# More seven-product quads, one weight split by an adding transfer, and a head that reads x already turned

## The chip, the cores and the metric

The kernel runs on one core of a Trainium2 chip. TensorE (PE) multiplies, VectorE (DVE), ScalarE (ACT) and GpSimd (POOL) work on tiles, SyncE (SP) issues most of the loads. The metric is the device time of one execution in microseconds. Three runs of the kernel before gave 2032.25, 2032.9 and 2036.04 us; the median is 2032.9 us.

## The reference, cut to what matters

One layer works on x of 256 tokens by 2048 numbers, in fp32. It has three stages, each of them a residual step:

```python
f = _swiglu(_rmsnorm(h, ln_ffn1_pre), ffn1_gate, ffn1_up, ffn1_down)   # (silu(u@gate) * (u@up)) @ down
h = h + 0.5 * _rmsnorm(f, ln_ffn1_post)
mx = _hybrid_mixer(_rmsnorm(h, ln_mix_pre), w_in, ..., w_out)          # RWKV branch, pooling branch, two gates
h = h + _rmsnorm(mx, ln_mix_post)
f = _swiglu(_rmsnorm(h, ln_ffn2_pre), ffn2_gate, ffn2_up, ffn2_down)
h = h + 0.5 * _rmsnorm(f, ln_ffn2_post)
```

The hidden width of both feed-forward stages is 5632, so gate and up are 2048 x 5632 and down is 5632 x 2048. The mixer reads x through `w_in` and ends with `w_out` (2048 x 2048).

## The kernel before, in words

**Three products for one.** Every fp32 matrix is used as a high and a low part of type fp32r. ACT casts a loaded weight tile `w` to its high part (`wH<-w`), DVE subtracts the high part from the tile (`wL<-w,wH`). The helper `mm3` (L264 to L266) then issues three matmuls of 128 x 128 by 128 x 512 for each product of a row block and a weight tile: high by high, high by low, low by high. The 256 tokens are two halves of 128, the accumulators are PSUM banks of 128 x 512.

**Pairs and quads.** A pair (`pair` in `seven`, fed by `feed`, L281 cast and L287 subtraction) is two k-tiles of one 512-column weight block for both halves: 4 products, 12 matmuls. A quad (`quad`, lines L506 to L534) takes two k-tiles of two column blocks at once, which would be 8 products, and computes them with 7 after Strassen and Winograd, 21 matmuls. For that it needs sums of weight tiles (`t<-w,w` L513, `t<-w,t` L517 and L521 on DVE, split into high and low at L530 and L534) and sums of the activations (`sums`, tiles `sf`, `sH`, `sL`), which are made once and used by all column blocks. Four products go into banks of their own (p1, p5, p6, p7, shown as `ms`), which `merge` adds into the results (`u<-ms,u` and `u<-mm,u`, L570).

**Which k-tiles are quads** is written in strings: `FAST` for each of the nine gate/up blocks (blocks 2 to 10 of 11; blocks 0 and 1 are plain), `DOWN` for the two column pairs of down, `OUT` for the pair of columns 1 and 2 of `w_out`. In a string, f is a plain pair of the first column block, l one of the last, q a quad.

**A planner sets the order.** `job`, `pe`, `run` and `play` hold a list of jobs with a duration, a due time and dependencies, play them once with the written durations while the program is built, and write the instructions of PE, ACT and DVE in the order that comes out. Loads go to SP's queue, the moves of the hidden tiles (`x<-T`, 16 per block) to POOL's. Staging tiles for loads (`w32`, four of them) and pairs of split tiles (`wH`, `wL`, five) are handed on in the plan: the next user waits until the job that gives a tile free is done. The hidden tiles of a gate/up block are gated by DVE (L905), turned in 32 x 32 pieces (L786), moved by POOL and at once cast and split (L809 on ACT, L813 on DVE) into `xH` and `xL`.

**The head.** The first block loads x in token layout; PE turns it (`tr<-ident,x`, L768, four 128 x 128 transposes at a time, after 12 transposes `warm<-ident`), ACT and DVE scale and split it out of PSUM. The vectors of gains are loaded in rows and turned by PE too (`pg`, `pr`). Part of the work that follows (`gemm_rest`, `gemm_tok`, the first half of `ev_pa`) is not in the plan; its order is left to the scheduler.

Of the kernel before, what the change touches and what calls it, by code (L numbers as in the profile page):

```python
# [18 lines left out]
P = 128  # L19
D = 2048  # L20
S = 256
# [19 lines left out]
WARM = 12  # L41
# [13 lines left out]
ROWS = [("ln_mix_pre", 16), ("ln_ffn2_pre", 16), ("mu", 26), ("w0", 8), ("a0", 8),  # L55
        ("k_k", 8), ("k_a", 8)]
ROWS2 = [("r_k", 8), ("gn_w", 8), ("gn_b", 8), ("pool_scale", 8)]
# [18 lines left out]
class Block:  # L76
# [43 lines left out]
    def job(s, eng, dur, fn, due=0.0, deps=(), take=None, give=(), lag=None,  # L120
            rel=0.0):
        s.n += 1
        n = Node(s.n, eng, dur, fn, due, LAG[eng] if lag is None else lag, give)
        n.ready = rel if eng != "D" else rel - 10
        for d in deps:
            s.link(d, n)
        if take:
            s.asks.setdefault(take, []).append(n)
        if eng != "P":
            s.jobs.append(n)  # L130
        return n
# [14 lines left out]
    def run(s):  # L146
# [3 lines left out]
        for name, ns in s.asks.items():  # L150
            ns.sort(key=lambda n: n.due)
            wait[name] = deque(ns[CAPS[name]:])
            for n in wait[name]:
                n.left += 1
        order = deque(n for _, n in sorted(s.order, key=lambda o: o[0]))
        with s.tc.manual_schedule(engines={E.PE, E.Activation, E.DVE}):
            s.play(order, wait)
            s.stats()
        s.clk, s.order, s.asks, s.freed, s.jobs = 0.0, [], {}, {}, []

    def play(s, order, wait):

        free = dict(P=0.0, A=0.0, V=0.0, G=0.0, D=-10.0)
# [17 lines left out]
        def done(n, t):  # L181
            for name in n.give:
                if wait.get(name):
                    met(wait[name].popleft(), t)
# [83 lines left out]
    def feed(s, w, k, n, c0, t, hold=False):  # L268
# [3 lines left out]
        def get():  # L272
            b["w"] = s.get_w(w, k, n, c0, 512)

        def high():
            if hold:
                b["H"], b["L"] = s.unit(dt=F32R, p="kH"), s.unit(dt=F32R, p="kL")
            else:
                b["H"], b["L"] = [s.wp.tile([P, 1024], F32R, tag=g, name=s.nm(g), bufs=WS_BUFS)
                                  for g in ("wH", "wL")]  # L280
            s.nc.scalar.copy(b["H"][:, :m], b["w"][:, :m])  # L281
# [4 lines left out]
        def low():  # L286
            s.nc.vector.tensor_tensor(out=b["L"][:, :m], in0=b["w"][:, :m],  # L287
                                      in1=b["H"][:, :m].bitcast(F32), op=ALU.subtract)
        g = s.job("D", 1.75 * m / 1024, get, t - 9, take="w")
        h = s.job("A", aa(m), high, t - va(m) - aa(m) - 0.5, (g,), None if hold else "ws")  # L290
        return b, s.job("V", va(m), low, t - va(m) - 0.3, (h,), give=("w",))
# [10 lines left out]
    def gemm(s, w, c0, at, k0, k1, KT, evac, names, kd=lambda k: (), pss=None):  # L302
# [9 lines left out]
        for k in range(k0, k1, 2):  # L312
            b, l = s.feed(w, k, 2, c0, s.clk)
            e = s.pe(12 * MM, lambda k=k, b=b: do(k, b),
                     (l, *kd(k), *kd(k + 1), *(s.open(*names) if k == 0 else ())), ("ws",))
# [4 lines left out]
    def halves(s, w, c0, at, k0, k1, KT, names, pss, kd=lambda k, h: (), ends=None):  # L320

        fed, last = {}, None
        for k in range(k0, k1, 2):
            fed[k] = s.feed(w, k, 2, c0, s.clk + (k - k0) * 3 * MM, k - k0 >= 2 * WS_BUFS)
        for h in range(2):
            for k in range(k0, k1):
                b, l = fed[k // 2 * 2]

                def do(k=k, h=h, b=b):
# [3 lines left out]
                last = s.pe(3 * MM, do, (l, *kd(k, h), *(s.open(names[h]) if k == 0 else ())),  # L333
                            ("ws",) if h and k % 2 and k - k0 < 2 * WS_BUFS else ())
# [3 lines left out]
    def gemm_tok(s, w, c0, at, KT, evac, xs=None):  # L338

        pss = [s.pm.tile([P, 512], F32, tag="mm", name=s.nm("mm")) for _ in range(2)]  # L340
        ws = {}

        def do(k, h):
            (wH, wL), (xH, xL) = ws[k], at(k)
            s.mm3(pss[h], xH[:, h * P:h * P + P], xL[:, h * P:h * P + P], wH, wL,
                  k == 0, k == KT - 1)

        def keep(tiles):
            ws.update((k, (wH, wL)) for k, wH, wL in tiles)

        if xs:
            s.head(w, c0, KT, do, keep, xs)
        else:
            for k2 in range(0, KT, 4):
                keep(s.load_w(w, k2, min(4, KT - k2), c0, 512))
                for k in range(k2, min(k2 + 4, KT)):
                    do(k, 0)
                    do(k, 1)
        with s.tc.high_priority(offset=BOOST):
            for h in range(2):  # L360
                evac(h, pss[h])

    def lead(s, w, c0, at, KT, kd):
# [3 lines left out]
        s.run()  # L367
        return pss

    def gemm_rest(s, w, c0, at, KT, evac, pss):  # L370

        for k2 in range(STAG, KT, 4):
            ws = {k: t for k, *t in s.load_w(w, k2, min(4, KT - k2), c0, 512)}
            for k in range(k2, min(k2 + 4, KT)):
                for h in range(2):
                    (wH, wL), (xH, xL) = ws[k], at(k)
                    s.mm3(pss[f"f{h}"], xH[:, h * P:h * P + P], xL[:, h * P:h * P + P],
                          wH, wL, k == 0, k == KT - 1)
        with s.tc.high_priority(offset=BOOST):
            for h in range(2):  # L380
                evac(h, pss[f"f{h}"])

    def sums(s, src, sm, q0, nq, t, deps, own=None, hl=False):
# [1471 lines left out]
```

## Time and profile before

| | |
|---|---|
| median of three runs | 2032.9 us |
| the profiled execution, its own time | 2033.49 us |
| its span | 2031.8 us |
| PE busy | 2014.8 us (99%) |
| DVE busy | 1735.4 us (85%), 95.69 of the 100 us from 300 to 400 |
| ACT busy | 1164.7 us (57%) |
| POOL busy | 326.6 us (16%) |
| loads and stores | 423.55 MB, mean 208 GB/s |

The span is the stretch that the profiler shows, from the first to the last instruction; 1.7 us of the profiled execution's time lie outside it. Busy shares are of the span. DVE's share is an average over stages: the nine gate/up blocks with quads run from about 97 to 470 us and from about 1421 to 1795 us, down follows each of them, and the mixer lies between.

### The profile page before, as it was taken

How to read it: one execution, taken by the hardware profiler on the slowest of the kernel's cores; microseconds unless marked ns; L12 is line 12 of the kernel's file. 1: busy time of each engine (PE TensorE's matmuls, PEld its weight loads, DVE VectorE, ACT ScalarE, POOL GpSimd, SP SyncE). 2: the span in 40 equal slices, each digit the busy share in tenths (PEclk: the TensorE clock that was granted, in tenths of full speed). 3: DMA queues.
4: the chain of work that ended last, by engine and by line, in shares of the span. 5: the costliest groups of instructions: out<-in, count | busy, mean ns of one | idle time of the engine just before them, and what ended most of it. 6: DMA issues, size and time to landing. Idle time of an engine off the chain costs nothing.

```text
span 2031.8 us, 28759 instructions
## 1 busy us (share of the span) xinstructions
PE 2014.8 (99%) x10011; PEld 1664.1 (82%) x10011; DVE 1735.4 (85%) x2300; ACT 1164.7 (57%) x1559; POOL 326.6 (16%) x673
## 2 busy tenths in 40 slices
PE   9999999999999999999999999999999999999997
PEld 7888888888888888888788788888888878888886
DVE  6989999988998857789689577769999989989986
ACT  7555565555565566685575444565565555555653
POOL 0121112211000023403220111012211122110000
PEclk9999999999999999999999999999999999999999
DMA  7666676766667777757456557676666767666674
GB/s 261 205 198 218 217 220 203 226 201 221 208 207 253 233 210 215 205 176 215 144 176 183 161 171 271 209 219 192 213 211 216 222 190 232 201 221 209 205 258 146
DMA packets 226842, 423.55 MB, mean 208 GB/s; under 512 B 24063, under 2 KB 27529, under 8 KB 226697
## 3 DMA queue, kind: packets, MB, share of 16 engines
q1 hardware_dynamic: 204137, 384.70, 60.8%
q0 software_dynamic: 22272, 36.51, 5.5%
q8 instruction: 78, 1.28, 0.3%
q10 hardware_dynamic: 288, 0.52, 0.1%
q14 instruction: 67, 0.55, 0.1%
HBM read 396.69 MB, written 8.39 MB: 199 GB/s over the span
## 4 chain that ended last, share of the span: by engine, by line
PE 97%; issue 1%; DMA 1%; DVE 1%; ACT 1%; POOL 0%; DVEq 0%; POOLq 0%; SPq 0%; ACTq 0%
PE mm L264 27%; PE mm L266 27%; PE mm L265 27%; PE ms L266 4%; PE ms L265 4%; PE ms L264 4%; PE tr L768 1%; DMA x<-T 0%; PE pA L1575 0%; PE mc L728 0%; PE pU L1671 0%; DMA w<-in_ffn_gate_dram 0%; PE pSa L1683 0%; PE pY L1706 0%; PE pT L1742 0%
## 5 line engine op out<-in xcount | busy, mean ns | idle before, releaser
L264 PE MATMUL mm<-wH,xH 128*128 128x512 f32 (+1 forms) x2232 | 871.6, 391 | 0.0
L266 PE MATMUL mm<-wH,xL 128*128 128x512 f32 (+1 forms) x2232 | 866.5, 388 | 0.6 <-DVE xL L777 0.5
L265 PE MATMUL mm<-wL,xH 128*128 128x512 f32 (+1 forms) x2232 | 866.6, 388 | 0.2
L281 ACT CAST wH<-w 128x1024 fp32r<-128x1024 f32 x373 | 388.1, 1053 | 231.3 <-PE mm L266 139.5
L287 DVE TENSOR_TENSOR wL<-w,wH 128x1024 fp32r<-128x1024 f32 x373 | 449.4, 1221 | 77.8 <-ACT wH L281 72.0
L266 PEld LDWEIGHTS mm<-wH,xL 128*128 128x128 f32 x2232 | 419.0, 188 | 87.9 <-DVE xL L777 2.3
L264 PEld LDWEIGHTS mm<-wH,xH 128*128 128x128 f32 x2232 | 419.1, 188 | 86.4 <-ACT xH L772 0.2
L265 PEld LDWEIGHTS mm<-wL,xH 128*128 128x128 f32 x2232 | 419.3, 188 | 85.1 <-DVE wL L287 1.0
L530 ACT CAST wH<-t 128x1024 fp32r<-128x1024 f32 x172 | 181.1, 1053 | 221.9 <-DVE t L521 113.1
L797 POOL DMA_DIRECT2D x<-T x352 | 173.1, 499 | 735.2 <-issue 299.0
L241 DVE TENSOR_TENSOR wL<-w,wH 128x1024 fp32r<-128x1024 f32 (+3 forms) x178 | 209.9, 1188 | 82.7 <-ACT wH L240 81.2
L240 ACT CAST wH<-w 128x1024 fp32r<-128x1024 f32 (+3 forms) x178 | 182.1, 1027 | 149.7 <-PE mm L266 129.3
L534 DVE TENSOR_TENSOR wL<-t,wH 128x1024 fp32r<-128x1024 f32 x172 | 205.9, 1219 | 14.3 <-ACT wH L530 13.6
L530 ACT CAST wH<-w 128x1024 fp32r<-128x1024 f32 (+1 forms) x172 | 143.1, 834 | 70.7 <-PE mm L266 32.5
L534 DVE TENSOR_TENSOR wL<-w,wH 128x1024 fp32r<-128x1024 f32 (+1 forms) x172 | 163.7, 952 | 5.2 <-ACT wH L530 5.0
L513 DVE TENSOR_TENSOR t<-w,w 128x1024 f32<-128x1024 f32 x86 | 105.0, 1220 | 12.2 <-DMA w<-in_ffn_down_dram 7.6
L570 DVE TENSOR_TENSOR u<-mm,u 128x512 f32<-128x512 f32 x92 | 61.1, 683 | 11.0 <-PE mm L266 11.0
L265 PE MATMUL ms<-wL,sH 128*128 128x512 f32 x174 | 67.9, 390 | 1.4 <-DVE wL L534 1.4
L264 PE MATMUL ms<-wH,sH 128*128 128x512 f32 x174 | 67.8, 390 | 1.0 <-ACT wH L530 1.0
L266 PE MATMUL ms<-wH,sL 128*128 128x512 f32 x174 | 67.7, 389 | 0.0
L570 DVE TENSOR_TENSOR u<-ms,u 128x512 f32<-128x512 f32 x92 | 61.3, 687 | 1.6
L809 ACT CAST xH<-x 128x512 fp32r<-128x512 f32 x44 | 26.8, 617 | 62.4 <-DMA x<-T 59.5
(332 smaller groups left out, 2064.4 us busy)
## 6 DMA issues: line engine op xcount, KB each, us to landing
w<-in_w_in_dram SPq DMA_DIRECT2D x128, 512.0 KB
w<-in_ffn_up_dram SPq DMA_DIRECT2D x122, 512.0 KB
w<-in_ffn_gate_dram SPq DMA_DIRECT2D x120, 512.0 KB
w<-in_ffn_down_dram SPq DMA_DIRECT2D x116, 512.0 KB
w<-in_ffn_down_dram SPq DMA_DIRECT2D x120, 256.0 KB
w<-in_ffn_gate_dram SPq DMA_DIRECT2D x112, 256.0 KB
w<-in_ffn_up_dram SPq DMA_DIRECT2D x108, 256.0 KB
w<-in_w_out_dram SPq DMA_DIRECT2D x28, 512.0 KB
```

The source lines that it names most:

```text
L240: s.nc.scalar.copy(vH, v)
L241: s.nc.vector.tensor_tensor(out=vL, in0=v, in1=vH.bitcast(F32), op=ALU.subtract)
L264: nc.tensor.matmul(ps, aH, bH, start=start, stop=False)
L265: nc.tensor.matmul(ps, aH, bL, start=False, stop=False)
L266: nc.tensor.matmul(ps, aL, bH, start=False, stop=stop)
L281: s.nc.scalar.copy(b["H"][:, :m], b["w"][:, :m])
L287: s.nc.vector.tensor_tensor(out=b["L"][:, :m], in0=b["w"][:, :m], in1=b["H"][:, :m].bitcast(F32), op=ALU.subtract)
L513: V.tensor_tensor(out=v["t13"], in0=v["a"], in1=v["b0"].to_broadcast([P, 2, 512]), op=ALU.subtract)
L530: nc.scalar.copy(x[n_][0], v[n_])
L534: V.tensor_tensor(out=L, in0=v[n_], in1=H.bitcast(F32), op=ALU.subtract)
L570: V.tensor_tensor(out=u[o], in0=pss[b], in1=u[i], op=ALU.add)
L797: nc.gpsimd.dma_start(out=x[0][q * 32:q * 32 + 32, i], in_=src[i * 32:i * 32 + 32, q])
```

## The change

**The strings.** Each gate/up block has four quads in place of three and so four pairs of each column block in place of five. Down's first pair has eight quads in place of seven; its second keeps eight. The output's pair has four in place of two. Plain pairs and quads stand in another order. In all that is 18 quads more in gate/up (nine blocks, two feed-forward stages), two in down and two in the output.

**The adding transfer.** A capital F in a string is a plain pair whose low part is not made by DVE. ACT casts the tile to its high part (`high`), then writes minus the tile into the low tile, whose type rounds it to minus the high part (`minus`), and POOL issues a transfer that adds the tile itself into the low tile (`add`). ACT's first pass is planned `AHEAD` = 9 us before the pair is due. There is one in each of the 18 blocks, one in down's first pair in each stage, one in the output's.

**The hidden tiles** are only moved in the gate/up blocks. Their cast and split (L809, L813 before) is done in down, shortly before the first use of each, and `sums` of down read the moved tile itself in place of high plus low.

**More tiles.** `run` takes a list `MORE` of further staging and split tiles, out of the pool of units, that may be handed on until a written time of the plan (400 in the first plan, 550 in the last).

**The head.** The program gets two further arrays, x with the feature axis first and all gain vectors as columns, so PE turns neither. The token-layout x is still loaded, later, for the sum of squares. There are 26 warm transposes.

**More in the plan.** The rest of each stage's first block and the projection `w_proj_a` (`plan_pa`) are planned jobs; the RWKV steps have a written wait of the same size and another layout of one small tile.

```diff
-WARM = 12
+WARM = 26
+AHEAD = 9.0
...
+MORE=(dict(w=(400,)*2, ws=(400,)*3), dict(w=(550,)*2, ws=(550,)*3))
-FAST = {b: "fffqffqllqlll" for b in range(2, 11)}
-DOWN = ((0, "fffffffffqffffqfflqlllqllqllqllqlllll", 0),
+FAST = {b: "Ffqffqlqqlll" for b in range(2, 11)}
+DOWN = ((0, "fffflFlqffqflqllllqfqlfqllllqffqffll", 0),
         (2, "fffqffqffqffqffqffqflqllqlll", TRAIL))
-OUT = ((0, "", 0), (1, "fffffqflqlllll", 0), (3, "", TRAIL))
+OUT = ((0, "", 0), (1, "lqfqlqfqFfll", 0), (3, "", TRAIL))
...
+    def feed_add(s, w, k, c0, t):
...
+        def high():
+            b["H"], b["L"] = s.room(b["ws"] is not None)
+            s.nc.scalar.copy(b["H"], b["t"])
...
+        def minus():
+            s.nc.scalar.activation(out=b["L"], in_=b["t"], func=AF.Copy, scale=-1.0)
+
+        def add():
+            s.nc.gpsimd.dma_start(out=b["L"], in_=b["t"], accum_op=ALU.add)
+        g = s.job("D", 1.75, get, t - AHEAD - 9, take=("w", b))
+        h = s.job("A", aa(1024), high, t - AHEAD, (g,), ("ws", b))
+        m = s.job("A", aa(1024), minus, t - AHEAD + 0.1, (h,))
+        a = s.job("G", 0.93, add, t - AHEAD + 1.5, (m,), lag=0.0)
+        return b, s.job("D", 3.2, lambda: None, t - AHEAD + 2, (a,), give=(("w", b),))
...
+                by, c = (s.feed_add if c.isupper() else s.feed), c.lower()
...
+        if hX is not None:
+            return s.job("N", 0, None, 0, ms)
+        return s.split(lambda: x[0], hT, b, t + 10.5, (ms,))
...
+        def part(k):
+            H, L = [u[:, k % 4] for u in uT[k // 4]]
+            v = xT[k // 4][:, k % 4]
+            nc.scalar.activation(out=H, in_=v, func=AF.Copy, scale=g[:, k:k + 1])
+            nc.vector.scalar_tensor_tensor(out=L, in0=v, scalar=g[:, k:k + 1],
+                                           in1=H.bitcast(F32), op0=ALU.mult,
+                                           op1=ALU.subtract)
```

**The order at three places.** First PE's first rows, the head: `warm` is the warm-up, `tr` a turned piece of x, `mm` the two accumulators of the first gate block. Before:

```order
L636 MATMUL warm_124<-ident 128x128 x12
L1781 MATMUL pg_37_140<-ident,g1rows_89 128x16
L768 MATMUL tr_173<-ident,x_85 128x128 x4
L768 MATMUL tr_190<-ident,x_87 128x128 x4
L264 MATMUL mm_120<-wH_169,xH_91 128x512
L265 MATMUL mm_120<-wL_170,xH_91 128x512
L266 MATMUL mm_120<-wH_169,xL_92 128x512
L264 MATMUL mm_121<-wH_169,xH_91 128x512
L265 MATMUL mm_121<-wL_170,xH_91 128x512
L266 MATMUL mm_121<-wH_169,xL_92 128x512
L768 MATMUL tr_217<-ident,x_85 128x128 x4
```

and now:

```order
L649 MATMUL warm_134<-ident 128x128 x26
L273 MATMUL mm_217<-wH_191,xH_95 128x512
L274 MATMUL mm_217<-wL_192,xH_95 128x512
L275 MATMUL mm_217<-wH_191,xL_96 128x512
L273 MATMUL mm_221<-wH_191,xH_95 128x512
L274 MATMUL mm_221<-wL_192,xH_95 128x512
L275 MATMUL mm_221<-wH_191,xL_96 128x512
L273 MATMUL mm_217<-wH_197,xH_95 128x512
```

The turns of x are gone from PE's queue, there were eight rows of four, and the warm-up is 14 transposes longer.

Second DVE in the middle of a gate/up block: `wL<-w` are low parts of pairs and quads, `t` the weight sums of a quad, `xL` low parts of hidden tiles. Before, a quad, the split of a hidden tile and a pair:

```order
L513 TENSOR_TENSOR t_2600_2341<-w_2583_2277,w_2586_2289 128x1024
L534 TENSOR_TENSOR wL_2325<-w_2583_2277,wH_2324 128x1024
L517 TENSOR_TENSOR t_2601_2342<-w_2583_2277,t_2600_2341 128x512
L534 TENSOR_TENSOR wL_2360<-w_2586_2289,wH_2359 128x512
L521 TENSOR_TENSOR t_2601_2342<-w_2586_2289,t_2601_2342 128x512
L534 TENSOR_TENSOR wL_2363<-t_2600_2341,wH_2362 128x1024
L813 TENSOR_TENSOR xL_2385<-x_2582_2258,xH_2384 128x4x128
L534 TENSOR_TENSOR wL_2388<-t_2601_2342,wH_2387 128x1024
L813 TENSOR_TENSOR xL_2385<-x_2582_2258,xH_2384 128x4x128
L287 TENSOR_TENSOR wL_2403<-w_2597_2328,wH_2402 128x1024
```

and now, the last two quads of a block and the first pairs behind them:

```order
L515 TENSOR_TENSOR t_2795_2342<-w_2767_2211,w_2774_2253 128x1024
L534 TENSOR_TENSOR kL_2314<-w_2767_2211,kH_2313 128x1024
L519 TENSOR_TENSOR t_2796_2343<-w_2767_2211,t_2795_2342 128x512
L534 TENSOR_TENSOR kL_2352<-w_2774_2253,kH_2351 128x512
L523 TENSOR_TENSOR t_2796_2343<-w_2774_2253,t_2796_2343 128x512
L534 TENSOR_TENSOR kL_2356<-t_2795_2342,kH_2355 128x1024
L515 TENSOR_TENSOR t_2809_2402<-w_2781_2274,w_2788_2310 128x1024
L534 TENSOR_TENSOR wL_2383<-t_2796_2343,wH_2382 128x1024
L519 TENSOR_TENSOR t_2810_2403<-w_2781_2274,t_2809_2402 128x512
L534 TENSOR_TENSOR wL_2369<-w_2781_2274,wH_2368 128x1024
```

Two quads follow each other directly, the hidden tiles' splits are gone from here, and some split tiles (`kH`, `kL`) are the further ones out of the pool of units.

Third ACT, around the pair with the adding transfer at a block's start:

```order
L292 CAST kH_1670<-w_2622_1576 128x1024
L313 CAST kH_1677<-w_2621_1559 128x1024
L292 CAST kH_1687<-w_2629_1599 128x1024
L319 ACTIVATE kL_1678<-w_2621_1559 128x1024
L292 CAST wH_1704<-w_2634_1621 128x1024
L292 CAST wH_1714<-w_2641_1654 128x1024
```

and POOL in the same stretch:

```order
L781 DMA x_2516_1096<-T_2513_1077 32x256 x16
L322 DMA wL_1296<-w_2531_1150 128x1024
L781 DMA x_2599_1471<-T_2598_1467 32x256 x16
L322 DMA kL_1678<-w_2621_1559 128x1024
```

The two ACT passes of the pair (L313, L319) have another pair's cast between them. On POOL's queue each adding transfer (L322) stands behind the sixteen moves of one block's hidden tile and ahead of the next block's.

More of the change, by code (lines that the diff above doesn't have):

```diff
@@ L40 @@
 TRAIL = 16
-WARM = 12
+WARM = 26
+AHEAD = 9.0
+FILL = 19.5
+FILB = 5
 TB = 4
@@ L144, in pe, with run @@
         return n
-    def run(s):
+    def run(s, more={}, busy=0.0):
         E = mybir.EngineType
@@ L181, in done @@
         def done(n, t):
[L182 to L184 removed]
+            for name, b in n.give:
+                if wait.get(name) and (b[name] is None or t < b[name]):
+                    m, b2 = wait[name].popleft()
+                    b2[name] = b[name]
+                    met(m, t)
             for k in n.kids:
```

621 lines of the change are left out of this document (311 added, 310 removed).

## The prediction

> **What bounds the kernel now.** I read the page's busy shares and its chain of waits first, then PE's own waits, then single stretches.
>
> ```profile
> span 2031.8 us, 28759 instructions
> PE 2014.8 (99%) x10011; PEld 1664.1 (82%) x10011; DVE 1735.4 (85%) x2300; ACT 1164.7 (57%) x1559; POOL 326.6 (16%) x673
> ...
> PE 97%; issue 1%; DMA 1%; DVE 1%; ACT 1%; POOL 0%; DVEq 0%; POOLq 0%; SPq 0%; ACTq 0%
> ```
>
> PE is 97% of the chain that ended last: time is the number of matmuls times their pitch. PE's waits, all of them in this view:
>
> ```profile
> PE warm L636 <- POOL ident masks.py:199: 1.7, 1, 1.7
> PE ms L265 <- DVE wL L534: 1.4, 2, 0.8
> PE ms L264 <- ACT wH L530: 1.0, 1, 1.0
> PE pS L1691 <- ACT R L1685: 0.7, 1, 0.7
> PE mm L266 <- DVE xL L777: 0.5, 1, 0.5
> PE tr L768 <- DMA x<-in_x_dram: 0.2, 1, 0.2
> ```
>
> Outside the head PE waits 3.1 us in all. The pitch, from PE's timeline of a plain block:
>
> ```profile
> 61.38 0.39 PE L264 MATMUL mm<-wH,xH 128*128 128x512 f32 x1
> ...
> 72.27 0.39 PE L264 MATMUL mm<-wH,xH 128*128 128x512 f32 x1
> ```
>
> The second stands 48 matmuls behind the first: 10.89 / 48 = 0.227 us each (the 0.39 overlaps the next).
>
> The cover is thin elsewhere, though. One gate/up block with three quads, first all engines (PE, weight loads, DVE, ACT, POOL, clock, DMA share), then DVE by form with mean time and idle time:
>
> ```profile
> 300.00:341.50 41.50, 41.50 (x185) 34.38 (x184) 39.61 (x46) 23.74 (x28) 7.85 (x16) 1.00 0.70 216
> ```
>
> ```profile
> L287 DVE TENSOR_TENSOR wL<-w,wH 128x1024 fp32r<-128x1024 f32 x10 | 12.0, 1220 | 0.8 <-ACT wH L281 0.5
> L534 DVE TENSOR_TENSOR wL<-t,wH 128x1024 fp32r<-128x1024 f32 x6 | 7.1, 1218 | 0.3 <-ACT wH L530 0.3
> ...
> L570 DVE TENSOR_TENSOR u<-ms,u 128x512 f32<-128x512 f32 x5 | 3.3, 686 | 0.1
> L570 DVE TENSOR_TENSOR u<-mm,u 128x512 f32<-128x512 f32 x4 | 2.6, 682 | 0.0
> ...
> L813 DVE TENSOR_TENSOR xL<-x,xH 128x512 fp32r<-128x512 f32 x2 | 1.4, 688 | 0.6 <-ACT xH L809 0.6
> ```
>
> DVE is busy 39.61 of 41.50 us: 1.89 us are left. Its pitch is shorter than its mean time, since ends overlap the next start:
>
> ```profile
> 265.14 1.28 DVE L570 TENSOR_TENSOR u<-mm,u 128x512 f32<-128x512 f32 x2
> ...
> 267.54 1.30 DVE L786 STREAM_TRANSPOSE T<-u 128x512 f32<-128x512 f32 x2
> ...
> 271.67 2.35 DVE L534 TENSOR_TENSOR wL<-t,wH 128x1024 fp32r<-128x1024 f32 x2
> ```
>
> Two less one: 2.35 - 1.22 = 1.13 us for 1024 numbers, 1.28 - 0.68 = 0.60 for 512, 1.30 - 0.69 = 0.61 for a turn.
>
> **The quads.** A quad has 21 matmuls for the 24 of two pairs. The strings add 18 in gate/up, 2 in down, 2 in the output: 22 x 3 = 66 matmuls, 66 x 0.227 = **15.0 us** off PE. Nothing on PE is added for them: the merges per column pair stay as many.
>
> **DVE in a block.** Before: 22 passes of 1024 (10 pairs, 4 in each of 3 quads), 21 of 512 (3 in each quad, 8 merges, 2 gates, 2 hidden splits), 2 turns: 22 x 1.13 + 21 x 0.60 + 2 x 0.61 = 38.7 us against PE's 183 x 0.227 = 41.5. After: 7 pairs (the eighth is the adding transfer's) and 16 in quads make 23 passes, 12 + 8 + 2 of 512, 2 turns: 26.0 + 13.2 + 1.2 = **40.4 us against PE's 180 x 0.227 = 40.9**. PE's gain shows only if DVE hardly waits: 0.5 us are left where 2.8 were by the same count. What DVE now waits for is mostly ACT, and ACT in turn for a split tile that PE still holds:
>
> ```profile
> L281 ACT CAST wH<-w 128x1024 fp32r<-128x1024 f32 x373 | 388.1, 1053 | 231.3 <-PE mm L266 139.5
> ...
> L809 ACT CAST xH<-x 128x512 fp32r<-128x512 f32 x44 | 26.8, 617 | 62.4 <-DMA x<-T 59.5
> ```
>
> That is what more tiles take away: up to five further ones are handed on until 400 and 550 us of the plans, so ACT and the loads run ahead and DVE finds its input ready. ACT has room: the quad's casts (3 x 1.05 + 0.62) less two pairs' (2.1), plus the adding pair's second pass (1.05), less two hidden casts (1.2) are 1.5 us on 23.74, and ACT no longer stops in a block for a hidden tile that is still moving. Bounds for what stays: nothing, if DVE's waits fall under the 0.5 us; 40.4 + 1.89 = 42.3 us per block, 1.4 over PE, if all of today's waits stay, 18 x 1.4 = 25 us. Five of the six rows' waits are on casts and so of the kind that the tiles remove; I take 0.2 us per block, 4 us.
>
> **Down** gets the hidden tiles' splits: 22 passes of 0.60 = 13.2 us of DVE in its first pair, plus a quad (4 x 1.13 + 3 x 0.60 = 6.3) less three pair passes (3.4) and less the four joins (4 x 1.13, the `sx` row) that `sums` no longer makes: about 12 more. The pair has 8 x 21 + 28 x 12 = 504 matmuls, 114.4 us, and the stretch had some 7% free (below it the output's):
>
> ```profile
> L394 DVE TENSOR_TENSOR sx<-xH,xL 128x1024 f32<-128x1024 f32 x9 | 11.0, 1218 | 0.0
> ```
>
> ```profile
> 500.00:600.00 100.00, 100.00 (x443) 82.81 (x442) 93.09 (x111) 58.50 (x72) 0.57 (x1) 1.00 0.63 205
> ...
> 1200.00:1300.00 100.00, 100.00 (x455) 83.05 (x454) 78.46 (x93) 49.68 (x61) 12.20 (x24) 1.00 0.69 230
> ```
>
> By busy time 107 + 12 is over 114; by pitch it fits, since every wait leaves some 0.09 us of overlap counted as busy. The splits of late tiles can lie anywhere ahead of their use. I take 0.5 us per stage, 1 in all (nothing to 5 each). In the output the stretch from 1200 to 1300 has DVE at 78%, so its two quads cost nothing there; without that cover 2 x 6.3 less 4 x 1.13 is 8 us.
>
> **The adding transfer** replaces a 1.13 us pass on DVE by an ACT pass and a POOL issue. No transfer of before adds. The nearest: transfers of the same queue, with time to landing:
>
> ```profile
> x<-T POOLq DMA_DIRECT2D x352, 32.0 KB, 3.9
> ...
> h<-hsp POOLq DMA_DIRECT2D x8, 512.0 KB, 9.2
> ...
> mb<-msp POOLq DMA_DIRECT2D x4, 512.0 KB, 6.0
> ```
>
> It starts 9 us ahead; two casts of 1.05 and the issue (0.55) leave 6.4 us plus what ACT is early. By the 6.0 row it is in time, by the 9.2 row (four issued together) 2.8 us late. Only the pair's second matmul waits for it. Late, it would hold all behind it on PE, 21 times. I take in time: single transfers of 512 KB are nearer to the 6.0 row, and ACT runs ahead. Its 21 x 0.5 MB are 2.6% of 423.55 MB at a DMA share of 0.70. POOL's 16 moves of a block (16 x 0.5 us) stand ahead of it on its queue, but are due half a block earlier.
>
> The Trainium skill, "DMA: Bandwidth & Descriptors", section Rules for kernel authors, says that an accumulating DMA reads its destination and writes it later, so it moves more than a plain one. By the same page's fit (Anatomy of one DMA: 2.0 us plus bytes over 436 GB/s) 512 KB take 3.2 us, and with another read an estimated 4.4, in time as well; the 6.0 and 9.2 us rows are longer than the fit.
>
> **The head.** PE's timeline of it:
>
> ```profile
> 1.72 2.82 PE L636 MATMUL warm<-ident 128*128 128x128 f32 x12 [1.72 <-POOL ident masks.py:199]
> ...
> 6.75 0.78 PE L264 MATMUL mm<-wH,xH 128*128 128x512 f32 x1
> ...
> 9.69 0.60 PE L768 MATMUL tr<-ident,x 128*128 128x128 f32 x4
> 10.05 0.48 PE L264 MATMUL mm<-wH,xH 128*128 128x512 f32 x1
> 10.37 0.39 PE L265 MATMUL mm<-wL,xH 128*128 128x512 f32 x1
> ...
> 33.12 0.40 PE L264 MATMUL mm<-wH,xH 128*128 128x512 f32 x1
> ```
>
> The gate block's 96 matmuls run from 6.75 to 33.12, 26.4 us for 96 x 0.227 = 21.8: six turns of 0.36 + 0.09 each (9.69 to 10.05, and the next matmul 0.32 after instead of 0.23), six slow matmuls at the start (2.94 for 1.36). After there are no turns, so the stretch is 21.8. It begins when 26 warm transposes end: at 2.82 / 12 = 0.235 each at 7.8 us; at half of that once they are fast, as matmuls are after 10.05, near 6.6. So the gain is 3.5 to 4.7; I take **4 us**. The loads can follow: between 5 and 10 us they ran at
>
> ```profile
> 5.00:10.00 5.00, 4.31 (x17) 2.81 (x16) 3.38 (x11) 4.24 (x12) 0.00 (x0) 1.00 1.02 381
> ```
>
> 381 GB/s, and a k-tile brings 0.39 MB per 1.36 us, 290 GB/s. The 2 MB of token-layout x stand behind the gate weights.
>
> The Trainium skill, "TensorE: Matmul & The Clock Gate", section Part 1, gives about 3.4 us of sustained work until the array runs at full clock; by that the 26 transposes cover the slow part and 6.6 holds. The slow pitch up to 9.69 us here, behind a warm-up with gaps, agrees.
>
> **Sum.** Span 2031.8 - 15.0 - 4 + 4 + 1 = 2017.8. The profiled execution took 1.7 us more than its span, and the median of the runs is 0.6 below that execution: 2018.9, so **2019 us**.
>
> **Rivals.**
>
> *DVE becomes the bound.* Place: the 18 blocks. Each wait of DVE beyond 0.5 us per block comes out on PE. At all of the 1.89 a block takes 42.3 us against 41.5 before, 18 x 0.8 = +14; the other four quads (-2.7) and the head (-4) leave +7.7, **2041 us, slower**. It turns from faster to slower at 1.5 us kept per block ((41.5 + 6.7/18) - 40.4). For it: 95% busy in the stretch, and today's merges of a block's end wait for PE whatever the tiles. Against: the waits are on casts. Chance 0.18, of which a third ends on each side and a third within no change.
>
> *The adding transfer lands late.* 1 us late on 21 pairs is 21 us and takes all back: 2040. For it the 9.2 row and that it reads twice; against it that ACT is early. Chance 0.08, about half of it slower.
>
> *Better than the sum.* No new waits at all, and the 2.4 us of waits at `ms` gone with the new order: 2012. Chance 0.08.
>
> *It doesn't save what it says*, because something hides the matmuls: nothing on the chain does, 97% is PE; I give it nothing beside the three.
>
> **Numbers.** The forecast (2014 to 2026) has 0.66. Faster by over 0.2% (4 us): 0.66 + 0.08 + 0.04 = 0.78; within 0.2%, what this measurement cannot tell from no change: 0.11; slower: 0.11. The range leaves out the upper half of the slower cases and the best ones: 2012 to 2034.
>
> **What would show it.** PE: 66 fewer 512-column matmuls, no `tr<-ident,x`, the up block's first matmul near 28.5 us. DVE: busy over 97% in the blocks, with few waits; its groups' idle time under 0.5 us per block. If DVE is the bound, PE waits for `wL` at L534 or for a bank that a merge frees at a block's start. If the transfer is late, PE waits at the second matmul of one pair per block for a DMA. Wrong would be a gate/up block that takes 41 us or more, or a head that ends after 30 us.

## The result, and the profile after

The changed kernel takes 2016.86 us (median of four runs, 2016.07 to 2018.06), the kernel before 2032.58 beside it: a ratio of 0.9919, 95% interval 0.9902 to 0.9937. The profiled execution's span went from 2031.8 to 2015.2 us, 16.6 less, where the sum of the prediction gave 14.0 less. The medians and the spans tell the same.

From the profile's page, the span, the busy shares and the engines' shares of the chain that ended last:

```profile
span 2015.2 us, 28638 instructions
PE 1996.1 (99%) x9924; PEld 1647.0 (82%) x9924; DVE 1780.3 (88%) x2385; ACT 1207.9 (60%) x1611; POOL 342.4 (17%) x692
PE 88%; DVE 7%; issue 2%; DMA 1%; ACT 1%; SPq 0%; POOL 0%; DVEq 0%; POOLq 0%; ACTq 0%
```

PE still sets the end, but the chain now passes through DVE for 7% where it was 1%: PE and DVE are level in the blocks. PE's waits in the changed kernel (in all, times, longest):

```profile
PE warm L649 <- POOL ident masks.py:199: 1.7, 1, 1.7
PE mm L273 <- ACT wH L249: 1.3, 2, 1.0
PE mm L274 <- DVE wL L250: 1.0, 2, 0.8
PE ms L274 <- DVE wL L534: 0.9, 2, 0.6
PE pS L1712 <- ACT R L1706: 0.7, 1, 0.7
PE mm L275 <- DVE xL L759: 0.6, 2, 0.3
```

The two waits at L249 and L250 are in the head and new; none is in a gate/up block. One such block, all engines (columns as in the prediction), and its two largest DVE groups (busy, mean ns, then idle time before them):

```profile
300.00:340.90 40.90, 40.90 (x183) 33.85 (x182) 40.81 (x48) 25.03 (x28) 8.83 (x17) 1.00 0.76 232
```

```profile
L534 DVE TENSOR_TENSOR wL<-t,wH 128x1024 fp32r<-128x1024 f32 x7 | 8.4, 1218 | 0.0
L515 DVE TENSOR_TENSOR t<-w,w 128x1024 f32<-128x1024 f32 x4 | 4.9, 1217 | 0.0
```

DVE is busy 40.81 of 40.90 us, and its groups' idle time, up to 0.8 us in the kernel before, is 0.1 us at the most. PE has 66 matmuls of 512 columns fewer (8316 for 8382), as forecast.

Where the 16.6 us lie is read from PE's timeline. Before: the mixer's first `pn`, its last `pg`, the output's last transposes, the last matmul.

```profile
862.45 0.72 PE L1492 MATMUL pn<-bones,R 128*128 128x2 f32 x6
1191.07 0.28 PE L1733 MATMUL pg<-lgs,wH 128*128 128x256 f32 x1
1335.68 0.60 PE L768 MATMUL tr<-ident,fg 128*128 128x128 f32 x4
2020.23 0.39 PE L266 MATMUL mm<-kH,xL 128*128 128x512 f32 x1
```

After, with the up block's first matmul (33.12 before) ahead of them:

```profile
31.22 0.39 PE L273 MATMUL mm<-wH,xH 128*128 128x512 f32 x1
855.08 1.84 PE L1513 MATMUL pn<-bones,R 128*128 128x2 f32 x16
1182.08 0.28 PE L1754 MATMUL pg<-lgs,wH 128*128 128x256 f32 x1
1325.54 0.60 PE L750 MATMUL tr<-ident,fg 128*128 128x128 f32 x4
2002.30 0.39 PE L275 MATMUL mm<-kH,xL 128*128 128x512 f32 x1
```

| stretch | before, us | after, us | change | matmuls saved x 0.227 |
|---|---|---|---|---|
| head, to the up block's first matmul | 33.1 | 31.2 | -1.9 | |
| first feed-forward stage | 829.3 | 823.9 | -5.4 | -6.8 |
| mixer | 328.6 | 327.0 | -1.6 | |
| output | 144.6 | 143.5 | -1.1 | -1.4 |
| second feed-forward stage | 684.6 | 676.8 | -7.8 | -6.8 |
| from the last matmul to the end | 11.6 | 12.9 | +1.3 | |

The sum is -16.5; by the count of matmuls the quads account for -15.0 of it. The rest are small terms of both signs, and it is these that the experiments turn to, beside the question why DVE no longer waits.

### The profile page after: what moved, and what is told of

It is laid out like the page before. It is cut to its first block, busy times and chain, and to the rows that moved or that the text cites. A ratio compares the mean times of both kernels' runs of the same rounds, so it can differ in the third digit from the quotient of the medians.

```text
span 2015.2 us, 28638 instructions
## 1 busy us (share of the span) xinstructions
PE 1996.1 (99%) x9924; PEld 1647.0 (82%) x9924; DVE 1780.3 (88%) x2385; ACT 1207.9 (60%) x1611; POOL 342.4 (17%) x692
## 4 chain that ended last, share of the span: by engine, by line
PE 88%; DVE 7%; issue 2%; DMA 1%; ACT 1%; SPq 0%; POOL 0%; DVEq 0%; POOLq 0%; ACTq 0%
PE mm L273 24%; PE mm L275 24%; PE mm L274 24%; PE ms L274 4%; PE ms L275 4%; PE ms L273 4%; DVE wL L534 2%; DVE wL L298 2%; DMA w<-in_ffn_down_dram 1%; DVE t L515 1%; DVE xL L807 1%; PE pA L1596 0%; DVE xL L759 0%; DVE t L523 0%; DMA w<-in_ffn_gate_dram 0%
## 5 line engine op out<-in xcount | busy, mean ns | idle before, releaser
L273 PE MATMUL mm<-wH,xH 128*128 128x512 f32 (+1 forms) x1726 | 674.8, 391 | 1.3 <-ACT wH L249 1.3
L274 PE MATMUL mm<-wL,xH 128*128 128x512 f32 (+1 forms) x1726 | 669.4, 388 | 1.0 <-DVE wL L250 1.0
L275 PE MATMUL mm<-wH,xL 128*128 128x512 f32 (+1 forms) x1726 | 669.4, 388 | 0.6 <-DVE xL L759 0.6
L298 DVE TENSOR_TENSOR wL<-w,wH 128x1024 fp32r<-128x1024 f32 x247 | 296.3, 1218 | 52.5 <-ACT wH L292 51.4
L250 DVE TENSOR_TENSOR wL<-w,wH 128x1024 fp32r<-128x1024 f32 (+2 forms) x159 | 188.2, 1192 | 74.4 <-ACT wH L249 73.0
L249 ACT CAST wH<-w 128x1024 fp32r<-128x1024 f32 (+2 forms) x159 | 162.7, 1026 | 135.4 <-PE mm L275 113.2
L534 DVE TENSOR_TENSOR wL<-t,wH 128x1024 fp32r<-128x1024 f32 x162 | 195.2, 1217 | 3.6 <-ACT wH L530 3.3
L273 PE MATMUL mm<-kH,xH 128*128 128x512 f32 x410 | 160.1, 390 | 0.0
L275 PE MATMUL mm<-kH,xL 128*128 128x512 f32 x410 | 159.6, 389 | 0.0
L274 PE MATMUL mm<-kL,xH 128*128 128x512 f32 x410 | 159.5, 389 | 0.0
L534 DVE TENSOR_TENSOR wL<-w,wH 128x512 fp32r<-128x512 f32 (+1 forms) x165 | 153.3, 929 | 1.8 <-ACT wH L530 1.7
```

Of the source, the lines that this page charges most:

```text
L249: s.nc.scalar.copy(vH, v)
L250: s.nc.vector.tensor_tensor(out=vL, in0=v, in1=vH.bitcast(F32), op=ALU.subtract)
L273: nc.tensor.matmul(ps, aH, bH, start=start, stop=False)
L274: nc.tensor.matmul(ps, aH, bL, start=False, stop=False)
L275: nc.tensor.matmul(ps, aL, bH, start=False, stop=stop)
L298: s.nc.vector.tensor_tensor(out=b["L"][:, :m], in0=b["t"][:, :m], in1=b["H"][:, :m].bitcast(F32), op=ALU.subtract)
```

## Experiments

Each kernel is the changed one with the edit shown; "span" is that of its profiled execution.

### What took DVE's waits away: quads and further tiles, two by two

```diff
-FAST = {b: "Ffqffqlqqlll" ...}            # three quads: this line alone
+FAST = {b: "fffqffqllqlll" ...}
-MORE=(dict(w=(400,)*2, ws=(400,)*3), dict(w=(550,)*2, ws=(550,)*3))
+MORE=({}, {})                             # no further tiles: this line alone; the fourth corner: both
```

Three quads:

> The changed kernel with the gate/up blocks at three quads and no adding transfer again (the other parts stay: further tiles, down, output, head). Theory 'a quad is worth its three matmuls, and nothing waits in the blocks': 18 x 3 x 0.227 = 12.2 us come back, span 2015.2 + 12.2 = 2027.4, median near 2029. Rival 'DVE already takes part of a quad's gain': the loss is under 10 us, span under 2025. A gate/up block then takes 41.5 us, with DVE near 38.7 by pitch.

No further tiles:

> The changed kernel without the further tiles (none handed on in either plan), the rest as it is. Theory 'the tiles took DVE's waits away': the waits on casts return, 1.0 to 1.9 us per block (DVE idle 1.89 of 41.5 before), so a block takes 41.4 to 42.3 against 40.9, 9 to 25 us, span 2024 to 2040. Rival 'the mixed order of pairs and quads alone does it': under 3 us, span under 2018.5, DVE idle under 0.5 us per block.

Three quads and no further tiles:

> The changed kernel with three quads per block, no adding transfer there, and no further tiles: the fourth corner beside the changed kernel (four quads, tiles), three quads with tiles (span 2032.7) and four quads without (2070.5). Theory 'four quads hold more tiles than three, so it is only with four that the further tiles count for much': the tiles are worth 0 to 15 us at three quads, span 2033 to 2048, against 55 at four. Rival 'the new order needs the tiles whatever the quads': 40 us or more here too, span over 2072.

| | three quads | four quads |
|---|---|---|
| with further tiles | 2034.6 (span 2032.7) | 2016.86 (span 2015.2) |
| without | 2039.77 (span 2036.2) | 2074.39 (span 2070.5) |

By its string a block with three quads has no adding transfer either, so the two columns differ by that too. Ratios to before: three quads 1.0008 (0.9999 to 1.0018), four quads without tiles 1.0203 (1.0188 to 1.0218), neither 1.0034 (1.0022 to 1.0046). So by the spans the tiles are worth 55 us with four quads and 3.5 with three, and a fourth quad without them costs 34 where it gains 17.5 with them (in the two feed-forward stages alone: costs 37, gains 12). By stages the tiles are worth 47 us with four quads and nothing with three (the stages are 2.6 us shorter without them); the other 9 and 6 us lie in the output, which has the same four quads in all four kernels. 340 us of the first stage's blocks, columns as above: the changed kernel, then three quads, four without further tiles, three without.

```profile
125.00:465.00 340.00, 340.00 (x1502) 281.63 (x1501) 336.63 (x392) 210.39 (x240) 70.30 (x136) 1.00 0.74 227
```

```profile
125.00:465.00 340.00, 340.00 (x1501) 281.63 (x1501) 310.25 (x353) 186.60 (x210) 62.59 (x128) 1.00 0.66 209
```

```profile
125.00:465.00 340.00, 326.52 (x1402) 260.16 (x1401) 320.11 (x368) 201.03 (x227) 70.24 (x136) 1.00 0.72 218
```

```profile
125.00:465.00 340.00, 340.00 (x1502) 281.53 (x1501) 316.18 (x357) 193.50 (x214) 62.69 (x128) 1.00 0.70 215
```

The count of PE's instructions tells the rate: with three quads PE never stops, tiles or not. With four and no further tiles it does 1402 in the time of 1502, 100 x 0.227 = 22.7 us behind, and DVE is not full either (320 of 340). The two largest of PE's waits in that kernel:

```profile
PE ms L274 <- DVE wL L534: 15.8, 33, 2.4
PE mm L274 <- DVE wL L534: 12.0, 16, 1.3
```

Both are on quads' split tiles. By the code a quad holds two loaded tiles, two of sums and four split ones, where the two pairs that it replaces hold two loaded and two split. With the common tiles alone the loads come late: in the same 340 us ACT waits 43.6 us for them and DVE 17.3 us for ACT's casts, where the changed kernel shows 7.3 and 3.3. The theory of the prediction (the tiles took the waits away) holds for four quads. The bound that I had drawn from it, at most 25 us if all of today's waits stay, does not: it took DVE's idle time of an order with three quads for one with four. With three DVE stands 30 us idle with the tiles and 24 without, and PE loses nothing by it. What is not separated is the adding transfer, which also holds a loaded tile and which only the four-quad blocks have: no run has four quads with neither it nor the tiles.

With three quads the two feed-forward stages take 5.0 and 7.3 us longer than in the changed kernel, 12.3 for a predicted 12.2: a quad, with the transfer that makes room for it on DVE, is worth its three matmuls. Another 7 us came from the mixer and the output, which the edit does not touch; they are taken up below.

### What the adding transfer is worth, and whether it lands in time

None at all (every F an f); a second one per block; five quads with four of them; and each planned 6 us later:

```diff
-"Ffqffqlqqlll"   "fffflFlqff..."   "lqfqlqfqFfll"
+"ffqffqlqqlll"   "ffffflqff..." with f for F   "lqfqlqfqffll"      # none: 21 plain pairs
+"FfqFfqlqqlll"                                                     # two per block
+"FfqFqqLqqLl"                                                      # five quads, four of them
-AHEAD = 9.0
+AHEAD = 3.0                                                        # planned later
```

> The changed kernel with every adding transfer turned back into a plain pair (21 in all), four quads per block kept. Theory 'DVE sets the block as soon as its passes by pitch are more than PE's': 24 x 1.13 + 22 x 0.60 + 2 x 0.61 = 41.5 us of DVE against 40.9 of PE, so a block takes 41.5, 18 x 0.6 = 11 us, span 2026, and PE waits for wL or for a bank in each block. Rival 'the lead that the further tiles give hides it': under 3 us, span under 2018.5, no PE waits in the blocks.

> The changed kernel with a second adding transfer in each gate/up block: DVE by pitch 22 x 1.13 + 22 x 0.60 + 2 x 0.61 = 39.3 us against PE's 40.9, where it is 40.4 now. Theory 'DVE waits for nothing and PE sets the blocks already': the blocks stay at 40.9; only the waits at down's first pair (2.2 and 1.5 us in the changed kernel) can shrink, span 2011.5 to 2016. Rival 'another adding pair holds its split tile some 9 us longer, and the tiles are what is scarce': DVE stops for casts again as in the kernel with five quads, 0.5 to 2 us per block, span 2024 to 2050.

> The changed kernel with five quads per gate/up block and four of its six pairs with an adding transfer. PE: 177 x 0.227 = 40.2 us per block. DVE by pitch: 22 passes x 1.13 + 25 x 0.60 + 2 x 0.61 = 41.1. Theory 'DVE by pitch sets the block': 41.1 against 40.9 now, 18 x 0.2 = 4 us slower than the changed kernel, span 2019, DVE at 99% and PE waiting 0.9 us per block. Rival 'PE alone counts': 18 x 0.68 = 12.2 us faster, span 2003. Rival 'four adding transfers per block come late': 1 us for each of 72, over 2050, with PE waiting for a DMA at a pair's second matmul.

> The changed kernel with the adding transfers planned 3 us ahead of their pair instead of 9. In the changed kernel they land 2.3 to 6.2 us ahead of the pair's second matmul in the blocks, most 4.4 to 5.3. Theory 'started 6 us later they land 6 us later': some 1 us late for each of 17 and 3.6 for two, about 20 to 25 us in all, span 2035 to 2040, PE waits for a DMA at the pair's second matmul. Rival 'ACT runs ahead of its plan, so the start hardly moves': span under 2018.

*None*: 2031.58 us, ratio 0.9993 (0.9984 to 1.0003), span 2029.8. Of the 14.6 us on the span, 8 are in the feed-forward stages (3.3 and 4.8); the mixer takes 3.7 more and the output 4.8, the head and the end 2 less. The mixer's part is the order of its instructions, as shown below; the output's is a wait of 3.1 us for a moved tile, the one met again with three quads, and a slow stretch of PE behind it (last section). The stretch of blocks:

```profile
125.00:465.00 340.00, 338.91 (x1489) 278.64 (x1489) 339.78 (x394) 200.19 (x230) 62.63 (x128) 1.00 0.67 213
```

DVE is busy 339.78 of 340 us and PE 13 matmuls behind. DVE sets the time, as its count by pitch said; PE loses less than the expected 11 us because what DVE had in advance is used up first: from 125 to 370 us PE shows no wait, and from there to 465 us it waits three times for wL at L534.

*Two per block*: 2016.86 us, ratio 0.9924 (0.9907 to 0.9941), span 2015.3. The time is the same, but the stages are not: the two feed-forward stages take 2.4 and 1.9 us more than in the changed kernel, and the end behind the last matmul 3.7 less. In the blocks PE runs as before up to 464 us: with one transfer DVE already waits for next to nothing, so a pass less gives PE nothing. What is lost lies at the end of the last block and at down's first quads. The rival (tiles held too long) did not show in the blocks; whether it is behind the loss at down was not tried.

*Five quads with four*: 2087.87 us, ratio 1.0278 (1.0259 to 1.0298), span 2078.4. None of the three theories fits. DVE was not full (315.89 of 340 us in the same stretch); the time is in the range of "late", over 2050, but PE waited for a transfer's landing only 1.3 us. SP did wait, for adding transfers, ahead of its loads: in this kernel (first two rows of four) and in the changed one.

```profile
SPq L508 <- DMA wL<-w: 94.6, 21, 9.5
SPq L508 <- DMA kL<-w: 46.2, 11, 9.4
```

```profile
SPq L508 <- DMA wL<-w: 45.7, 11, 6.3
SPq L508 <- DMA kL<-w: 11.7, 3, 4.0
```

An adding transfer reads the loaded tile until it lands, so that tile comes free for the next load some 7 us later than behind a DVE pass. One wait is no longer than in the changed kernel at the mean, some 4.2 us, but there are 75 transfers in place of 21, and ACT now waits for loads in a block (3.6 and 2.5 us in one). This was formed after the run. The experiments on down bear on it again; whether it is all of the 63 us, beside a fifth quad's own tiles, no run here tells. A part is the clock: for 13.6 us amid this run the granted clock was 0.5, as in the last section, which takes up to 6.8 us.

*Planned later*: 2020.66 us, ratio 0.9941 (0.9926 to 0.9956), span 2018.7. The transfer's own times in the changed kernel, issue on POOL (16 of the 21; the other five, onto kL, alike) and landing of all:

```profile
L322 POOL DMA_DIRECT2D wL<-w x16: 894/913/923, 125.4 to 1775.7; - x16
DMA to landing us min/median/max: 4.6/6.8/9.4
```

With these, paired with the first matmul that reads the tile, all 21 transfers of the changed kernel land in time: 2.3 us ahead at the least, 5.1 at the median. Planned 6 us later, they are 1.4 us ahead at the median, so 3.7 nearer to their use and not 6 (by the code a due time only chooses among jobs that are ready, and a free engine takes what is ready early). Four come late:

```profile
PE mm L274 <- DMA wL<-w: 3.7, 4, 2.3
```

These are close to the 3.5 us of the span, but by stages that is chance. Three of the four are in the feed-forward stages, 1.4 us together, and these stages are even 1.8 us shorter than in the changed kernel, since the waits at down's first quads are not there. The output is 4.8 us longer. Its one transfer came 2.3 us late, PE waited 0.6 us for a bank later on, and in between the granted clock (third last figure) fell to half, which costs 1.7 us:

```profile
1283.90:1287.30 3.40, 3.40 (x9) 2.65 (x8) 1.92 (x3) 0.66 (x1) 0.53 (x1) 0.50 0.96 316
```

So the first theory had the place of the waits right and the size not: 3.7 us for 20 to 25. The Trainium skill, "DMA: Bandwidth & Descriptors", section Anatomy of one DMA, has a fit by which 512 KB take 3.2 us, and an estimated 4.4 with a second read; the 6.8 us measured here are longer than both, and it is the measurement by which AHEAD has to be set.

### Down and the output

Down's first pair and the output's as before; down's alone as before; that with a late eighth quad; and that with an adding transfer in the eighth pair:

```diff
-DOWN[0] "fffflFlqffqflqllllqfqlfqllllqffqffll"   OUT[1] "lqfqlqfqFfll"
+DOWN[0] "fffffffffqffffqfflqlllqllqllqllqlllll"  OUT[1] "fffffqflqlllll"    # both as before
+DOWN[0] "fffffffffqffffqfflqlllqllqllqllqlllll"                             # down as before
+DOWN[0] "fffffffffqffffqflqlllqllqllqllqlqlll"                              # late eighth quad
+DOWN[0] "fffffffFfqffffqflqlllqllqllqllqlqlll"                              # and an adding transfer
```

> The changed kernel with the orders of down's first pair and of the output's pair as before (four quads fewer in all, their three adding transfers gone). Theory 'a quad is worth its three matmuls there too': 4 x 0.68 = 2.7 us slower, less the 2 to 4 us that PE now waits in down's first pair if these come from the eighth quad: span 2014 to 2018. Rival 'the old orders leave the hidden tiles' splits without cover': PE waits for wL in down's first pair over 5 us, span over 2022.

> The changed kernel with only the order of down's first pair as before (seven quads, the first behind nine plain pairs, no adding transfer), the output's new order kept. Theory 'only down's new order costs, the output's two quads pay': with both orders old the stretch from the mixer's last gate matmul to the last transpose of the output takes 144.9 us, with the new ones 143.8, so 2012.9 - 1.1 = 2011.8 for the span, median near 2013.4. Rival 'the output's new order costs too, in the stage behind it': 2013 or more for the span.

> As the kernel with down's old order, but with an eighth quad in it, late, and the first quad still behind nine plain pairs; no adding transfer in down. Theory 'PE's 3.7 us of waits in down come from the early quad, whose weights are not there yet (DVE waited 2.25 us for them)': the eighth quad then pays 2 x 0.68 = 1.4 us, span 2010.4. Rival 'down's first pair has no DVE time for an eighth quad beside the hidden tiles' splits': DVE over 99% in that pair, PE waits for wL late in it, span 2012.5 or more.

> The kernel with the late eighth quad in down's first pair, with one more change: its eighth plain pair gets an adding transfer. By this the scheduler puts DVE's instructions in the mixer in the order of the changed kernel again (word for word); with the late eighth quad alone they stood in the other order, that of the kernels with three quads and without adding transfers, and the mixer's stretch took 330.7 us where it took 327.0 with this one. Theory 'the 3.7 us are the mixer's order and nothing else, and the eighth quads pay 1.6 us': the stretch takes 327.0, span 2013.8 - 3.7 = 2010.1. Rival 'the stretch depends on what runs ahead of it, not on the order': it stays at 330, span over 2012.5. Rival 'an adding transfer that early in down comes late': PE waits for a DMA some 20 us into that pair, over 2011.5.

| kernel | median, us | ratio to before | span, us | first matmul of up to mixer | mixer |
|---|---|---|---|---|---|
| changed | 2016.86 | 0.9902 to 0.9937 | 2015.2 | 823.9 | 327.0 |
| both as before | 2014.5 | 0.9896 to 0.9925 | 2012.9 | 822.2 | 327.0 |
| down as before | 2013.15 | 0.9889 to 0.9916 | 2011.5 | 822.1 | 327.0 |
| late eighth quad | 2015.65 | 0.9902 to 0.9929 | 2013.8 | 821.4 | 330.7 |
| and adding transfer | 2017.56 | 0.9913 to 0.9940 | 2014.9 | 824.3 | 327.1 |

Down's new order takes back more than its quads bring: with the old one the span is 3.7 us shorter, though two quads are fewer (2.5 us of it in the two feed-forward stages, 0.8 in the head, which differs that much between kernels of one head). This is the fastest kernel of the study; its runs (2013.03 to 2013.39) and those of the changed one (2016.07 to 2018.06) do not overlap, while the intervals of the two ratios, each to its own runs of the kernel before, do.

What costs in down is seen at its first quad. In the changed kernel DVE waits there for a load, and PE behind it:

```profile
480.62 1.22 DVE L515 TENSOR_TENSOR t<-w,w 128x1024 f32<-128x1024 f32 x1 [2.25 <-DMA w<-in_ffn_down_dram]
```

```profile
486.07 0.50 PE L274 MATMUL ms<-wL,sH 128*128 128x512 f32 x1 [0.58 <-DVE wL L534]
```

I had put it down to the early place of that quad, and the kernel with a late eighth one agreed: no wait in down, and both stages shorter than with seven (0.7 and 1.0 us). Then an adding transfer two places ahead of the first quad, put there for another reason, brought PE's waits back, and the stages took 2.9 and 1.5 us longer, with no quad's place changed. SP's waits from 450 to 490 us in that kernel, then in the changed one, where F stands as close to the first quad:

```profile
SPq L235 <- DMA wL<-w: 6.4, 1, 6.4
```

```profile
SPq L508 <- DMA wL<-w: 6.3, 1, 6.3
```

In the three kernels of the table without an F in down SP has no such wait there. So the adding transfer just ahead of a quad costs time there, and SP's wait says how: it delays the quad's loads, by the tile that it holds. That the early place costs something beside is not excluded.

The late eighth quad was still slower as a whole than the kernel with seven, by 2.3 us, and that is the mixer:

```profile
852.00:1182.70 330.70, 327.06 (x2413) 265.31 (x2412) 263.56 (x478) 194.54 (x311) 64.83 (x113) 1.00 0.58 174
```

```profile
852.50:1179.50 327.00, 326.25 (x2414) 265.44 (x2413) 263.50 (x478) 194.26 (x310) 64.18 (x110) 1.00 0.59 176
```

The same work and 3.7 us more (late eighth quad, then seven quads). The mixer's code is the same, but DVE's instructions there (and ACT's with them) stand in one of two orders, equal row by row within each: one in the changed kernel, with down as before and with two adding transfers per block; the other with the late eighth quad, with three quads and without adding transfers. The last kernel here was made to get the first order back, and its mixer took 327.1: this part of its theory held. Its gain went into the wait above.

### The head

```diff
-WARM = 26
+WARM = 12
```

> The changed kernel with 12 warm transposes instead of 26. In the changed kernel the up block's first matmul starts at 31.2 us (30.3 to 30.7 in five other kernels with the same head), where 28.5 was predicted. Theory 'the loads set the head': the first matmul still starts near 7 us, the up block's still at 30.3 to 31.2, the time unchanged within 1 us. Rival 'the transposes set it': the first matmul starts up to 2 us earlier and the head ends 1 to 2 us earlier. Rival 'the clock': the first matmuls run slowly (over 0.3 us each, as in the kernel before) and the head ends 1 us later or more.

2018.48 us (2017.97 to 2019.49), ratio 0.9929 (0.9916 to 0.9943), span 2016.8; the up block starts at 31.6 us. The head of the changed kernel first, ACT's cast of the third k-tile and PE at it, then PE with 12 transposes.

```profile
9.92 1.05 ACT L249 CAST wH<-w 128x1024 fp32r<-128x1024 f32 x1 [0.82 <-DMA w<-in_ffn_gate_dram]
```

```profile
10.35 0.40 PE L275 MATMUL mm<-wH,xL 128*128 128x512 f32 x1
11.02 0.51 PE L273 MATMUL mm<-wH,xH 128*128 128x512 f32 x1 [0.26 <-ACT wH L249]
12.27 0.50 PE L274 MATMUL mm<-wL,xH 128*128 128x512 f32 x1 [0.75 <-DVE wL L250]
```

```profile
7.03 0.80 PE L273 MATMUL mm<-wH,xH 128*128 128x512 f32 x1 [2.50 <-ACT wH L249]
...
9.21 0.63 PE L274 MATMUL mm<-wL,xH 128*128 128x512 f32 x1
9.63 0.63 PE L275 MATMUL mm<-wH,xL 128*128 128x512 f32 x1
...
12.56 0.40 PE L273 MATMUL mm<-wH,xH 128*128 128x512 f32 x1
```

With 12 the first matmul starts hardly earlier (7.03 against 7.19): with both, ACT first waits for the load of x, to 5.96 and 6.12 us, and casts the weight behind it. The next ones run at 0.43 us each (9.21 to 9.63) until 12.2 us. With 26 they run at 0.23 from 8.3 us on, and PE catches up with the loads: it stands 0.4 us longer than a pitch at the third k-tile's first matmul and 1.0 at its second. So the loads set both heads; the slow matmuls cost little because they fill time in which PE would wait. Whether they cost anything is unclear: 1.6 us by the medians, with ranges that touch, and a head that ends 1.0 us after the median of the others (30.6) but level with the latest of them. The Trainium skill, "TensorE: Matmul & The Clock Gate", section Part 1, gives about 3.4 us of sustained work until full clock, counted in a window that does not start with the work. Here, after a gap of 2.5 us, it took 5.2 us (7.03 to 12.2), between one and two such windows.

## Why the prediction was right, and where its terms were off

The forecast of 2019 us (2014 to 2026) stands against 2016.86. Its reason held: time is PE's matmuls, if DVE does not wait.

- **The quads, -15.0.** Held. Three quads in place of four cost 12.3 us in the two stages for 12.2; in the output two brought 1.1 for 1.4.
- **DVE in a block, 40.4 against 40.9 by pitch.** Held: 40.81 busy of 40.90. Without adding transfers, at 41.5, DVE is full and PE falls behind.
- **New waits, +4 (0.2 per block; bounds 0 to 25).** Mis-sized: nothing at all in the blocks. The lower bound came true, and the upper one was no bound: without the tiles that I named as what takes the waits away, the same order loses 55 us. The waits of before belonged to an order that holds fewer tiles at once. (By its rows, three groups and not five had waited for casts, 1.4 of the 1.9 us.)
- **Down, +1.** Mis-sized, and for another reason than the hidden tiles' splits. Its old order is 2.5 us better in the two stages with 1.4 us of matmuls more, so the new one costs 3.8 there and not 1. I costed the F in down like one in a block, as nothing; there the next quad's loads wait for its tile, and with the late eighth quad the F alone cost 4.5 us in the two stages.
- **The adding transfer in time.** Held, with other numbers: 6.8 us to land and 0.92 to issue where I took 0.55, but ACT some 5 us earlier than planned (9.0 less two casts less 6.8, counted from the start of the issue, leaves 0.1 us; 5.1 were measured).
- **The head, -4.** Failed by half: -1.9. I said that the loads can follow, from a mean rate of 381 GB/s. They follow at the mean, but the first ones do not come when PE could use them: the transposes are done at 6.2 us and the first matmul starts at 7.19 where I had 6.6, it and the next lose 0.6 us more, and PE stands some 1.4 us at the third k-tile; the 28.5 us were not reached (30.3 to 31.6 in all kernels with this head), and by my own mark, over 30 us, this term was wrong.
- **Not seen:** the mixer's -1.6 and +1.3 at the end. With the other of its two orders the mixer would have come out some 2 us slower than before, so the gain hangs on an order that nobody chose; what its new code is worth beside that was not separated. Why the kernel ends 7.3 us after DVE's last instruction, and 6.0 before, was not tried; in the kernels of this study the end behind the last matmul takes from 9.2 to 12.9 us.
- **The rivals.** "DVE becomes the bound" did not come, but is one step away: one pass more per block, and it is there. "Late" needs a plan 6 us later to show. Of "better than the sum" one half came, no new waits in the blocks; of the 2.4 us of `ms` waits 0.9 are left, at a new place.

By stretches: the two feed-forward stages came out 4.6 us better than the sum (-13.6 for the quads, +4, +1, against -13.2), the mixer 1.6 better; the head 2.1 worse, the end 1.3, the output 0.3. That is 2.5 better in all, of errors that partly cancelled, so the 2 us between forecast and result are partly luck.

## What to carry to other kernels

When two engines are to be brought level, count the passes of the second by pitch, and see to it that its inputs lie ready: the fourth quad (with its adding transfer) gained 12 us in its stages with five further tiles and lost 37 without. Take no bound for a new order from the waits of an old one that needs fewer tiles at once. What replaces a pass by a transfer frees the engine but holds the source tile until the landing, so place it where the next loads do not need that tile.

## What the runs showed of the hardware and the program that I had not expected

A 512 KB adding transfer from tile to tile took 6.8 us at the median, no less than a plain load onto a tile by the same queue (the `mb<-msp` row: 6.0 before).

A wait of PE can cost more than it lasts. Behind the wait of 2.3 us in the output of the kernel planned later, and behind that of 3.1 us without adding transfers, the granted clock was 0.50 for 3.4 us and matmuls came every 0.43 us in place of 0.227, 1.7 us lost each time. Behind the 3.5 us below it was not, and matmuls kept 0.23 us; what decides it these runs do not tell.

An edit in one stage moved others by several microseconds. Two cases were seen: the two orders of DVE's instructions in the mixer (3.7 us), and POOL's queue at the output. With three quads, POOL's 16 moves of one tile are issued with waits between them; in the changed kernel without.

```profile
1212.25 2.48 POOL L781 DMA_DIRECT2D sga<-T  x5 [22.35 <-DVE T L768]
1217.38 3.91 POOL L781 DMA_DIRECT2D sga<-T  x8 [2.65 <-issue]
1222.55 0.50 POOL L781 DMA_DIRECT2D sga<-T  x1 [1.26 <-DMA sga<-T]
1225.05 0.50 POOL L781 DMA_DIRECT2D sga<-T  x1 [2.01 <-DMA sga<-T]
1226.23 0.50 POOL L781 DMA_DIRECT2D sga<-T  x1 [0.68 <-DMA sga<-T]
```

```profile
1204.17 7.84 POOL L781 DMA_DIRECT2D sga<-T  x16 [22.36 <-DVE T L768]
```

The 16 moves took 14.5 us to issue instead of 7.8, the cast of the moved tile came late, DVE stood behind it, and PE waited 3.5 us for a transpose:

```profile
1232.34 1.29 DVE L807 TENSOR_TENSOR xL<-sga,xH 128x512 fp32r<-128x512 f32 x2 [6.12 <-ACT xH L803]
```

```profile
PE tr L750 <- DVE sga L1352: 3.5, 1, 3.5
```

Why a move there waits for an earlier one's landing in the one kernel and not in the other stays open. It means that a difference of some 5 us between two versions of this kernel is read by stages, as here, before it is put down to the edit.
